# Three edits to a planned hybrid decoder kernel: at most four rows of x loaded ahead, a lead for the states' transposes, and head sums as two one-pass products

## The chip, the cores and the metric

The kernel runs on one core of a Trainium2 chip. A core has a matrix engine (TensorE, PE in the profile, with its weight loads as PEld), a vector engine (VectorE, DVE), an activation engine (ScalarE, ACT), a general engine (GpSimd, POOL), and a queue from which this kernel issues all its DMAs (SyncE, SP). The metric is the time of one execution in microseconds (us) on the device.

## What is computed

One layer of a hybrid decoder step, for a prompt of 1024 tokens and for 8 sample tokens with states of their own, with D = 1024:

```python
p = x @ w_in                                  # 1024 -> 3088 (GLA) + 4224 (RWKV) + 2048 (gates)
# GLA: 4 heads, keys of 128, values of 256: gated linear attention, norm, silu gate
S_t = diag(a_t) S_{t-1} + k_t^T v_t ; o_t = q_t S_t
# RWKV-7: 16 heads of 64, on p shifted by one token
kk = kb * k_k ; kk = kk / max(sqrt(sum(kk^2 over a head)), 1e-12)
S_t = S_{t-1} (diag(w_t) - kk_t^T (kk_t * a_t)) + v_t^T k_t ; y_t = S_t r_t
y = (y - mean(y)) * rsqrt(var(y) + eps) * lnx_w + lnx_b      # mean and variance over a head
bonus = sum(r * k * r_k over a head) * v
# merge
m = sigmoid(gate_a) * (o_gla @ w_up_gla) + sigmoid(gate_b) * (o_rwkv @ w_up_rwkv)
y_out = layernorm(alpha * x + m @ w_out)
```

Also returned are the states after the prompt, the samples' new states and the last projected rows. All tensors are float32.

## The kernel before, in words

The tokens are worked on in two passes of 520 (512 and the 8 samples, as two tiles of 260 columns) and 512 tokens. Activations lie feature by token: 128 features on the partitions, tokens along the columns. In each pass a plan of blocks runs through `w_in`, 128 output features a block: 8 slices of x by 3 products for each tile. Each float32 operand is split into a high part that TensorE takes in one pass (float32r) and the rest, and the products are high by high, high by low and low by high (`blocks`, L670 to L705). These are the products called `proj<-xh,whi`, `proj<-xl,whi` and `proj<-xh,wlo`, the input products of this text. Other products of full float32 operands go through TensorE in two passes, and the profile has two records for each.

After both passes come the products with `w_up_gla` and `w_up_rwkv` for each half, then `w_out` with the layer norm. At each of these changes of operand (a swap), the eight slices of x are replaced: `load_x` (L583) loads a slice into a buffer of the kind `row`, a cast on ScalarE makes the high part `xh` (`high`), a subtraction makes `xl` (`low`), and the row is freed. A slice can only be replaced after the last product that reads it, and the loads begin three blocks ahead (`AHEAD`). There are 26 `row` buffers of [128, 520] for everything: projected rows, GLA heads, RWKV pairs, samples, gates and x. A block that makes a projected row waits until a row is free beyond those that others wait for (`KEEP`, L57).

The RWKV heads are worked on in pairs, 8 a pass. A pair's `front` (L1027) makes decays, normalised keys, masked products (`big<-az,wide`) and the 32-step triangular solve on VectorE (`X`, `Xt`, over `LD` in DRAM); `back` and `turn` finish the inverse and transpose; `chain` (L1176) runs 8 dependent steps of small products (`pch<-wide,gg`, `pch<-rh,XT`, `pch<-wide`, and `pY`) with VectorE and ScalarE in between; `norm` (L1229) normalises. The sum over a head's 64 features is needed twice in `front` and twice in `norm`; `head_sums` (L461) is one float32 product with a block matrix of ones (`big<-row,cons`, 128 by 512). GLA heads (L752) do the same over 128 partitions with split operands already: `split` (L446) and `sums` (L453), the products `big<-part,onesr`. The samples' GLA states go through rows (`row<-state_gla`, `row<-vd`, stored as `gla_s`) and products `big<-row` of 8 columns (L886). The samples' RWKV step (L1249) begins with two transposes (`big<-cons,smp`); a pair's final state is transposed and stored by `state` (L1219, `big<-cons,Sp`).

The order is not written out by hand. Each piece of work is a stream, a generator of operations, and a planner (`run`, L357) picks operation after operation from all streams at build time: it prices each operation, keeps clocks for each engine and buffer, and takes the one with the lowest start time less a lead. The leads are the tables `PRIO` (engines other than TensorE) and `ON_PE` (L74 to L77). What comes out is one fixed order for each engine's queue; at run time each engine takes its queue strictly in order and waits on semaphores. So a late operand on one engine holds back all that stands behind it there.

Nearly all instructions go through one helper, so the profile gives them all the line L214; they are told apart by tile names.

Of the kernel before, what the change touches and what calls it, by code (L numbers as in the profile page):

```python
# [11 lines left out]
F32R = mybir.dt.float32r  # L12
# [8 lines left out]
P = 128  # L21
# [8 lines left out]
GH, GDK, GDV = 4, 128, 256  # L30
RH, RN = 16, 64
NPAIR = RH // 2
C = 64
# [22 lines left out]

KEEP = 1  # L57
AHEAD = 3
SPARE_ROWS = 8


# [12 lines left out]
PRIO = {"evacuate": 0.7, "pair": 0.4, "turn": 0.5, "chain": 0.5, "norm": 0.1, "x": 0.7, "lora": 0.2, "rank": -0.3,  # L74
        "head": 0.3, "gate": 0.05, "w": 0.3, "out": -0.1, "state": 0, "block": 0.0}
ON_PE = {"evacuate": 0.0, "pair": 0.15, "turn": 0.1, "chain": 0.15, "norm": 0.15, "x": 0.0, "lora": 0.15, "rank": 0.1,
         "head": 0.1, "gate": 0.06, "w": 0.0, "out": -0.03, "state": 0.0, "block": 0.0}  # L77

URGENT = 0.6
SIGMOID, EXP = "sigmoid_and_others", "natural_log_exp_and_others"  # L80
# [10 lines left out]

CST = {}
_o = 0
for _n, _w in [("ident", 128), ("gmask", 256), ("heads", 128)]:
    CST[_n] = (_o, _w)
    _o += _w
CST_W = _o
# [9 lines left out]
def constants():  # L107
    c = np.zeros((P, CST_W), np.float32)

    def put(name, v):  # L110
        o, w = CST[name]
        c[:, o:o + w] = v

    i = np.arange(P)
    put("ident", np.eye(P))
    put("heads", (i[:, None] // C) == (i[None] // C))
    s, t = i[:, None] % C, i[None, :] % C
    put("gmask", np.concatenate([s < t, s <= t], axis=1))
    lev = np.zeros((P, 64 * MASKED), np.float32)
    for n, m in enumerate(LEVELS[:MASKED]):  # L120
        ri = np.array([x for x in range(P) if (x // m) % 2 == 1])
        j = i[:, None]
        lev[:, 64 * n:64 * n + 64] = ((j // (2 * m)) == (ri[None, :] // (2 * m))) & ((j // m) % 2 == 0)
    return c, lev


class Op:
# [274 lines left out]
class Kern(Order):  # L402
# [57 lines left out]

    def head_sums(self, x):  # L461

        ps = yield from self.bank("big", [P, HT])
        yield self.P.matmul(ps, self.cst("heads"), x, start=True, stop=True)
        return ps

    def pvec(self, name, j):
# [4 lines left out]
    def setup(self):  # L472
        nc, a = self.nc, self.a
        E = mybir.EngineType
        self.es.enter_context(self.tc.manual_schedule(engines={E.PE, E.Activation, E.DVE, E.Pool, E.SP}))
        cp = self.pool("const")
        wp = self.pool("w", side="left")
        self.dr = self.pool("dr", space=DRAM)
        pp = self.pool("psum", space=PSUM)
        xp = self.pool("x", side="right")  # L480
        self.r1 = r1 = self.pool("work", side="left")
        for tag, bufs in BANKS.items():
            self.buffers(tag, bufs, lambda tag=tag, bufs=bufs: pp.tile([P, 512], F32, name=tag, bufs=bufs))
        for tag, (shape, bufs) in SBUF.items():
            dt = F32R if tag in PARTS else F32
            self.buffers(tag, bufs, lambda tag=tag, shape=shape, bufs=bufs, dt=dt:
                         r1.tile(shape, dt, name=tag, bufs=bufs))
        for tag, (shape, bufs) in WBUF.items():
            dt = F32 if tag == "wraw" else F32R
            self.buffers(tag, bufs, lambda tag=tag, shape=shape, bufs=bufs, dt=dt:  # L490
                         wp.tile(shape, dt, name=tag, bufs=bufs))
        for k in range(NK):
            for v in "hl":
                tag = f"x{v}{k}"
                self.buffers(tag, 1, lambda tag=tag: xp.tile([P, HALF], F32R, name=tag, bufs=1))
        nc.scalar.preload_act_table_set(EXP)
        self.cons = cp.tile([P, CST_W], F32, name="cons")
        self.pv = cp.tile([P, PV_W], F32, name="pv")
        self.ident = self.cst("ident")
        self.omu = cp.tile([P, NRC], F32, name="omu")  # L500
        self.oka = cp.tile([P, 8], F32, name="oka")
        self.nkk = cp.tile([P, 8], F32, name="nkk")
        self.bias = {}
        for n, v in [("glaeps", GLA_EPS), ("gneps", GN_EPS), ("lneps", LN_EPS), ("one", 1.0),
                     ("kkl", 0.5 * math.log(KK_SCALE))]:
            t = cp.tile([P, 1], F32, name="b_" + n)
            nc.vector.memset(t, v)
            self.bias[n] = t
        dbg = getattr(self, "dbg", {})
        self.o_gla = dbg.get("o_gla", None) or self.dr.tile([D, T], F32, name="o_gla")  # L510
        self.o_rwkv = dbg.get("o_rwkv", None) or self.dr.tile([D, T], F32, name="o_rwkv")
        self.sg = [[[self.dr.tile([P, PASS[i][1]], F32, name=f"sg{i}{n}{k}") for k in range(NK)] for n in range(2)]
                   for i in range(2)]
        self.mg = [[self.dr.tile([P, PASS[i][1]], F32, name=f"mg{i}{k}") for k in range(NK)] for i in range(2)]

        self.lev = cp.tile([P, 64 * MASKED], F32, name="lev")

        self.onesr = cp.tile([P, P], F32R, name="onesr")
        self.wa = cp.tile([P, NK * 16], F32, name="wa")
        self.alr = [cp.tile([96, HALF], F32R, name=f"alr{n}") for n in range(2)]  # L520
        self.gw2 = cp.tile([96, GH * GDK], F32R, name="gw2")
        self.GS = [cp.tile([P, GDV], F32, name=f"GS{h}") for h in range(GH)]

        self.smp = cp.tile([P, 4, NPAIR, NS], F32, name="smp")
        self.RS = self.dr.tile([4, NS, D], F32, name="RS")
        self.WA = self.dr.tile([2, NS, D], F32, name="WA")
        self.tail = cp.tile([P, NS + 1, NRC], F32, name="tail")
        self.carry = cp.tile([P, NRC], F32, name="carry")
        self.shT = cp.tile([P, NRC, NS], F32, name="shT")
        self.reset = cp.tile([P, HT], U8, name="reset")  # L530
        nc.vector.memset(self.reset, 1)
        nc.vector.memset(self.reset[:, ::C], 0)

        self.Sp = [cp.tile([P, C], F32, name=f"Sp{n}") for n in range(NPAIR)]
        for t in self.Sp:
            nc.gpsimd.memset(t, 0.0)

        for tag, n, bufs in (("az", 4 * HT, 2), ("XT", 2 * HT, 2), ("X1", HT, 1), ("As", 2 * HT, 1)):
            ts = [cp.tile([P, n], F32, name=f"{tag}{i}") for i in range(bufs)]
            for t in ts:  # L540
                nc.gpsimd.memset(t, 0.0)
            self.fixed(tag, ts)
# [9 lines left out]
    def load_constants(self):  # L552
        a, V, E = self.a, self.V, self.E
        yield from self.load("wa", self.S.dma_start(self.wa, a["wa"]))
        self.has.add("wa")
        row = yield from self.row()
        yield V.memset(row, 1.0)
        yield V.tensor_copy(self.onesr, row[:, :P])
        yield V.memset(row, 0.0)
        for t in self.alr:  # L560
            yield V.tensor_copy(t, row[0:96])
        self.has.add("alr")
        yield from self.load("pv", self.S.dma_start(self.pv, a["pv"]))
        yield from self.load("shift", self.S.dma_start(self.shT, a["shiftT"]))
        o = PV["mu"][0]
        yield V.tensor_scalar(self.omu, self.pv[:, o:o + NRC], -1.0, 1.0, ALU.mult, ALU.add)
        o = PV["ka"][0]
        yield V.tensor_scalar(self.oka, self.pv[:, o:o + 8], -1.0, 1.0, ALU.mult, ALU.add)
        o = PV["kk"][0]
        yield V.tensor_scalar(self.nkk, self.pv[:, o:o + 8], -1.0, None, ALU.mult)  # L570
        self.has.add("pv")
        yield from self.load("cst", self.S.dma_start(self.cons, a["cst"]))
        raw = row[0:96, :GH * GDK]
        for n in range(3):
            yield self.S.dma_start(raw[32 * n:32 * n + 16], a["gla_alpha_w2"])
        yield self.S.dma_start(self.lev, a["lev"])
        yield V.tensor_copy(self.gw2, raw)
        yield V.tensor_sub(self.gw2[64:96], raw[64:96], self.gw2[64:96].bitcast(F32))
        self.free(row)
        self.has.add("cst")  # L580


    def load_x(self, src, i, wait=None, low_rank=False):  # L583
# [25 lines left out]
        self.spawn(high(), "x")  # L609
        self.spawn(low(), "x")  # L610
        for k in range(NK):
            raw = yield from self.row(n)
            rows = slice(k * P, (k + 1) * P)
            yield from self.load(f"x{k}", self.S.dma_start(
                raw, src[k] if isinstance(src, list) else src[rows, base:base + n]))
            raws.append(raw)
# [996 lines left out]

def layout(i):
    f = np.ascontiguousarray
    cst, lev = constants()
    ch = lambda v: v.reshape(-1, P).T
    pv = np.concatenate([ch(i["rwkv_mu"][0]), ch(i["rwkv_w0"][0]), ch(i["rwkv_a0"][0]), ch(i["rwkv_k_k"][0]),
                         ch(i["rwkv_k_a"][0]), ch(i["rwkv_r_k"][0].reshape(-1)), ch(i["rwkv_lnx_w"][0]),
# [2 lines left out]
    x = np.concatenate([xp, xs], axis=0)  # L1622
    xT = f(np.concatenate([xp[:HT], xs, xp[HT:]], axis=0).T)
    return {
        "cst": cst, "lev": lev, "pv": f(pv), "xT": xT, "x": f(x), "w_in": f(i["w_in"][0]),
        "wa": f(i["w_in"][0][:, OFF_A:OFF_R].reshape(NK, P, 16).transpose(1, 0, 2).reshape(P, NK * 16)),
        "gla_alpha_w2": f(i["gla_alpha_w2"][0]), "state_gla": f(i["state_gla"]), "state_rwkv": f(i["state_rwkv"]),
        "shiftT": f(i["state_rwkv_shift"][0].reshape(NS, NRC, P).transpose(2, 1, 0)),
# [25 lines left out]
```

## Time and profile before

| what | us |
| --- | --- |
| median of 3 runs | 1686.61 |
| lowest and highest | 1685.98, 1691.09 |
| the profiled execution | 1687.94 |
| span of its instructions | 1686.2 |
| TensorE busy | 1628.7 |
| VectorE busy | 1184.6 |
| ScalarE busy | 830.7 |
| mean granted clock of TensorE | 0.986 |

In rows of groups of instructions stand the line, the engine, the operation, out<-in by the program's names, the tile's shape, the count, then the busy time in us, the mean ns of one, the idle time before them in us and what ended it. In rows of the timeline stand the start in us, the duration in us, the engine, the instruction, and in brackets the idle time of the engine before it and what ended that. A product's duration covers its whole way through the array, so neighbours overlap; what a product costs in a stream is the distance from its start to the next one's. `f32` stands in the rows for both kinds of float32. The granted clock is a share of full speed.

### The profile page before, as it was taken

The numbers are of one execution on the slowest core, as the hardware profiler recorded it, in microseconds if no ns is written. First come the engines' busy times: TensorE is split into PE (matmuls) and PEld (weight loads), VectorE is DVE, ScalarE is ACT, GpSimd is POOL, SyncE is SP. The second block draws the span as 40 slices with busy tenths as digits, with TensorE's granted clock in tenths as the row PEclk, the third lists the DMA queues.
The fourth block names the chain that finished last, engine by engine and source line by source line (L and its number), as shares of the span: only waits on it lengthen the run. The fifth ranks groups of instructions, "written<-read, shape, count | busy, mean of one in ns | idle before, by whom it ended". The sixth has DMA issues, their size and how long they took to land.

```text
span 1686.2 us, 29927 instructions
## 1 busy us (share of the span) xinstructions
PE 1628.7 (97%) x10322; PEld 1430.9 (85%) x10322; DVE 1184.6 (70%) x3114; ACT 830.7 (49%) x1974; POOL 86.0 (5%) x183
## 2 busy tenths in 40 slices
PE   8999999999999998999999999999989999999998
PEld 7899999999999996888878778778867889988786
DVE  6777876887688766757656477898728876656565
ACT  5456755664657465443634254526243656644210
POOL 1100000100000000000000000200000000000000
PEclk9999999999999999899999999999988999999999
DMA  9777675777587657545364625454642487788522
GB/s 291 246 228 231 217 215 152 227 246 218 160 245 228 216 158 237 170 119 174 101 206 123 186 73 176 152 163 156 202 145 67 114 275 221 236 278 278 182 78 87
DMA packets 311778, 315.26 MB, mean 187 GB/s; under 512 B 75347, under 2 KB 197084, under 8 KB 311628
## 3 DMA queue, kind: packets, MB, share of 16 engines
q1 hardware_dynamic: 311628, 313.36, 59.9%
q8 instruction: 82, 1.34, 0.3%
q14 instruction: 68, 0.56, 0.1%
HBM read 195.45 MB, written 117.82 MB: 186 GB/s over the span
## 4 chain that ended last, share of the span: by engine, by line
PE 73%; DVE 12%; DMA 7%; ACT 3%; issue 2%; SPq 2%; POOL 0%; POOLq 0%; DVEq 0%; ACTq 0%
PE proj L214 41%; PE big L214 21%; PE pY L214 7%; DVE row L214 4%; PE pch L214 4%; DMA wide<-LD 2%; SPq L214 2%; DVE X L214 2%; DVE Xt L214 2%; ACT row L214 1%; DVE wide L214 1%; DMA row<-state_rwkv 1%; DVE wlo L214 1%; DVE az L214 1%; DMA wraw<-w_up_gla 1%
## 5 line engine op out<-in xcount | busy, mean ns | idle before, releaser
L214 PE MATMUL proj<-xl,whi 128*128 128x260 f32 (+1 forms) x1928 | 637.5, 331 | 0.0
L214 PE MATMUL proj<-xh,whi 128*128 128x260 f32 (+1 forms) x1928 | 635.9, 330 | 0.0
L214 PE MATMUL proj<-xh,wlo 128*128 128x260 f32 (+1 forms) x1928 | 635.0, 329 | 0.0
L214 PEld LDWEIGHTS proj<-xh,wlo 128*128 128x128 f32 x1928 | 364.9, 189 | 29.9 <-issue 6.6
L214 PEld LDWEIGHTS proj<-xh,whi 128*128 128x128 f32 x1928 | 365.2, 189 | 28.5 <-issue 5.4
L214 PEld LDWEIGHTS proj<-xl,whi 128*128 128x128 f32 x1928 | 364.9, 189 | 28.6 <-issue 6.5
L214 DVE TENSOR_TENSOR row<-row 128x256 f32<-128x256 f32 (+6 forms) x326 | 161.7, 503 | 23.8 <-ACT row L214 11.8
L214 ACT CAST whi<-wraw 128x512 fp32r<-128x512 f32 x210 | 129.9, 622 | 95.7 <-PE proj L214 51.7
L214 DVE TENSOR_TENSOR wlo<-wraw,whi 128x512 fp32r<-128x512 f32 x205 | 141.0, 691 | 40.5 <-ACT whi L214 37.3
L214 ACT ACTIVATE row<-row 128x512 f32<-128x512 f32 (+4 forms) x229 | 138.4, 611 | 44.6 <-DVE row L214 26.3
L214 DVE TENSOR_TENSOR Xt<-X,wide 128x60 f32<-128x60 f32 (+24 forms) x496 | 105.4, 212 | 43.8 <-DMA wide<-LD 31.2
L214 ACT ACTIVATE row<-proj,omu 128x260 f32<-128x260 f32 (+1 forms) x99 | 54.1, 547 | 150.2 <-PE proj L214 149.9
L214 PE MATMUL big<-row 128*128 128x64 f32 (+4 forms) x712 | 115.6, 282 | 12.5 <-DVE row L214 11.5
L214 PEld LDWEIGHTS big<-row 128*128 128x128 f32 (+1 forms) x712 | 96.9, 193 | 23.3 <-DVE row L214 13.5
L214 ACT ACTIVATE s0p<-wide,pc 64x64 f32<-64x64 f32 x256 | 88.1, 344 | 52.7 <-DVE wide L214 48.5
L214 DVE TENSOR_TENSOR X<-X,Xt 128x60 f32<-128x60 f32 (+24 forms) x496 | 104.8, 211 | 11.9
L214 ACT COPY wide<-pch 64x64 f32<-64x64 f32 x221 | 45.5, 206 | 114.3 <-PE pch L214 110.4
L214 DVE SCALAR_TENSOR_TENSOR row<-proj,pv,row 128x259 f32<-128x259 f32 (+1 forms) x99 | 56.3, 569 | 49.7 <-ACT tail L214 33.7
L214 DVE SCALAR_TENSOR_TENSOR wide<-pch,pc,s0p 64x64 f32<-64x64 f32 x224 | 63.1, 282 | 38.3 <-PE pch L214 33.7
L214 POOL TENSOR_TENSOR row<-row 128x512 f32<-128x512 f32 (+7 forms) x43 | 45.5, 1059 | 794.4 <-ACT row L214 211.7
L214 ACT COPY row<-big 128x128 f32<-128x128 f32 (+7 forms) x165 | 46.7, 307 | 66.8 <-PE big L214 63.5
L381 ACT ACT_TABLE_LOAD x56 | 71.8, 1283 | 1.0
(254 smaller groups left out, 2560.6 us busy)
## 6 DMA issues: line engine op xcount, KB each, us to landing
wraw<-w_in SPq DMA_DIRECT2D x146, 256.0 KB
wh<-whi SPq DMA_DIRECT2D x146, 256.0 KB
wl<-wlo SPq DMA_DIRECT2D x146, 256.0 KB
whi<-wh SPq DMA_DIRECT2D x146, 256.0 KB
wlo<-wl SPq DMA_DIRECT2D x146, 256.0 KB
wide<-LD SPq DMA_DIRECT2D x64, 128.0 KB
wraw<-w_up_gla SPq DMA_DIRECT2D x32, 256.0 KB
wraw<-w_up_rwkv SPq DMA_DIRECT2D x32, 256.0 KB
```

What stands on the lines that cost most here:

```text
L214: ways.append((eng, lambda call=call: call(out, *args, **kw), price(eng, name, out, args, ins)))
L381: self.nc.scalar.preload_act_table_set(self.table)
```

## The change

Three edits.

First, `load_x` loads a row of x only while fewer than `RAWS` = 4 rows are loaded and not yet cast; the first load of all, at the start of pass 0, is exempt. Second, `ON_PE["state"]` goes from 0.0 to 0.1, which gives the streams `state`, `rwkv_sample` and `tails` a lead of 0.1 us on TensorE. Third, `head_sums` splits its operand into the two `part` buffers and forms the sum as two one-pass products with a block matrix of ones in float32r, `headsr`, which comes by a load of its own at the start.

```diff
+RAWS = 4
...
-         "head": 0.1, "gate": 0.06, "w": 0.0, "out": -0.03, "state": 0.0, "block": 0.0}
+         "head": 0.1, "gate": 0.06, "w": 0.0, "out": -0.03, "state": 0.1, "block": 0.0}
...
-for _n, _w in [("ident", 128), ("gmask", 256), ("heads", 128)]:
+for _n, _w in [("ident", 128), ("gmask", 256)]:
...
     def head_sums(self, x):
 
+        hi, lo = yield from self.split(x)
         ps = yield from self.bank("big", [P, HT])
-        yield self.P.matmul(ps, self.cst("heads"), x, start=True, stop=True)
+        yield from self.sums(ps, self.headsr, hi, lo)
+        self.free(hi, lo)
         return ps
...
-        raw = row[0:96, :GH * GDK]
+        raw, heads = row[0:96, :GH * GDK], (yield from self.row(P))
+        yield self.S.dma_start(heads, a["heads"])
...
-        self.free(row)
+        yield V.tensor_copy(self.headsr, heads)
+        self.free(row, heads)
...
         for k in range(NK):
+            yield lambda: k - len(his) < RAWS or low_rank and not i
             raw = yield from self.row(n)
```

Since the planner weighs all streams at every step, the order of all engines shifts from the first head sum on. Three places follow.

On TensorE in pass 1, before: a run of products without an input product, with the second transpose of the samples at its head, chain steps (`pch`, `pY`), one head sum (`big<-row,cons`) and the masked products of the next pair (`big<-az,wide`).

```order
L214 MATMUL proj<-xh_9626,wlo 128x512
L214 MATMUL big<-cons,smp 128x128
L214 MATMUL pY<-gg,wide 128x128
L214 MATMUL pch<-wide,gg 128x128
L214 MATMUL pY<-az_175,wide 128x128
L214 MATMUL pch<-rh,XT_179 128x128
L214 MATMUL pch<-wide 128x128
L214 MATMUL big<-row,cons 128x512
L214 MATMUL pY<-gg,wide 128x128
L214 MATMUL pch<-wide,gg 128x128
L214 MATMUL big<-az_176,wide 128x256
```

Now, on TensorE at the place where the samples' transposes stand: the two products of a head sum (`big<-part,headsr`) with input products between them, masked products between the chain steps, and the second transpose among input products.

```order
L215 MATMUL big<-part,headsr 128x512
L215 MATMUL proj<-xh_9650,wlo 128x512
L215 MATMUL proj<-xh_9659,whi 128x512
L215 MATMUL big<-part,headsr 128x512
L215 MATMUL proj<-xl_9668,whi 128x512
L215 MATMUL big<-az_177,wide 128x256
L215 MATMUL pY<-gg,wide 128x128
L215 MATMUL big<-az_177,wide 128x256
L215 MATMUL pch<-wide,gg 128x128
```

The sum became two rows with two input products between; the samples' transposes moved some 400 input products towards the front.

On TensorE near the end of pass 0, before: the last products of the GLA samples (`big<-row`, 8 columns).

```order
L214 MATMUL proj<-xl_292,whi 128x260
L214 MATMUL proj<-xh_280,wlo 128x260
L214 MATMUL proj<-xh_285,whi 128x260
L214 MATMUL proj<-xl_313,whi 128x260
L214 MATMUL proj<-xh_285,wlo 128x260
L214 MATMUL big<-row 128x8 x8
L214 MATMUL proj<-xh_198,whi 128x260
```

Now, one of the same kind on TensorE:

```order
L215 MATMUL proj<-xl_254,whi 128x260
L215 MATMUL big<-row 128x8 x2
L215 MATMUL proj<-xh_235,wlo 128x260
L215 MATMUL proj<-xh_241,whi 128x260
L215 MATMUL proj<-xl_256,whi 128x260
L215 MATMUL proj<-xh_241,wlo 128x260
L215 MATMUL proj<-xh_248,whi 128x260
L215 MATMUL proj<-xl_289,whi 128x260
L215 MATMUL proj<-xh_248,wlo 128x260
```

Eight sample products in one row became pairs with input products between them.

On SP at the swap to the first half of `o_gla`, before: the loads of x (`row<-o_gla`) stand far ahead of the store of the gate row `sg_122`, which is the next row after these.

```order
L214 DMA row<-o_gla 128x520 x8
L214 DMA LD_15816<-gg 32x8x32 x3
L214 DMA whi<-wh_1_9190 128x512
L214 DMA wlo<-wl_1_9223 128x512
L214 DMA whi<-wh_0_9345 128x512
L214 DMA wlo<-wl_0_9347 128x512
L214 DMA whi<-wh_1_9367 128x512
L214 DMA wlo<-wl_1_9369 128x512
L214 DMA wraw<-w_up_gla 128x4x128 x3
L214 DMA wide<-LD_15816 32x1024 x4
L214 DMA o_gla<-row 128x512 x2
L214 DMA row<-sg_92 128x520
```

Now, on SP at the same swap, the second four of them:

```order
L215 DMA LD_16310<-gg 32x8x32 x4
L215 DMA wraw<-w_up_gla 128x4x128
L215 DMA shift_p<-sto 33x128
L215 DMA row<-sg_93 128x520
L215 DMA wide<-LD_16310 32x1024
L215 DMA sg_122<-row 128x512
L215 DMA wide<-LD_16310 32x1024
L215 DMA row<-o_gla 128x520 x3
L215 DMA wide<-LD_16310 32x1024 x2
L215 DMA wraw<-w_up_gla 128x4x128
L215 DMA row<-o_gla 128x520
```

The last four rows of x moved behind the gate row's store and two of the loads of LD.

More of the change, by code (lines that the diff above doesn't have):

```diff
@@ L115, in constants @@
     put("ident", np.eye(P))
-    put("heads", (i[:, None] // C) == (i[None] // C))
     s, t = i[:, None] % C, i[None, :] % C
@@ L123, in constants @@
         lev[:, 64 * n:64 * n + 64] = ((j // (2 * m)) == (ri[None, :] // (2 * m))) & ((j // m) % 2 == 0)
-    return c, lev
+    return c, lev, ((i[:, None] // C) == (i[None] // C)).astype(np.float32)
 class Op:
@@ L518, in setup @@
         self.onesr = cp.tile([P, P], F32R, name="onesr")
+        self.headsr = cp.tile([P, P], F32R, name="headsr")
         self.wa = cp.tile([P, NK * 16], F32, name="wa")
@@ L1615, in layout @@
     f = np.ascontiguousarray
-    cst, lev = constants()
+    cst, lev, heads = constants()
     ch = lambda v: v.reshape(-1, P).T
@@ L1624, in layout @@
     return {
-        "cst": cst, "lev": lev, "pv": f(pv), "xT": xT, "x": f(x), "w_in": f(i["w_in"][0]),
+        "cst": cst, "lev": lev, "heads": heads, "pv": f(pv), "xT": xT, "x": f(x), "w_in": f(i["w_in"][0]),
         "wa": f(i["w_in"][0][:, OFF_A:OFF_R].reshape(NK, P, 16).transpose(1, 0, 2).reshape(P, NK * 16)),
```

## The prediction

> **What bounds the kernel now.** I read the page first: its engine row, then the slices.
>
> ```profile
> span 1686.2 us, 29927 instructions
> PE 1628.7 (97%) x10322; PEld 1430.9 (85%) x10322; DVE 1184.6 (70%) x3114; ACT 830.7 (49%) x1974; POOL 86.0 (5%) x183
> PE   8999999999999998999999999999989999999998
> PEclk9999999999999999899999999999988999999999
> DMA  9777675777587657545364625454642487788522
> ```
>
> TensorE (PE) is busy 97% of the span, nothing else more than 85%, and PE's nines run from start to end, so the time is PE's work plus the few places where PE waits or runs slowly. Busy shares of PE hide the second part, because its products overlap, so I looked for places where the granted clock falls (it does so only after waits) and asked for the busy times there, first of everything, then of products into `proj` alone. Columns: stretch, its length, busy us of PE, PEld, DVE, ACT, POOL with counts, granted clock, DMA share, GB/s.
>
> ```profile
> 670.40:686.40 16.00, 9.12 (x42) 8.62 (x41) 13.73 (x57) 6.10 (x14) 0.00 (x0) 0.57 0.38 129
> 962.30:978.60 16.30, 13.54 (x73) 10.84 (x71) 5.66 (x10) 8.57 (x17) 0.00 (x0) 0.79 0.15 41
> 985.10:998.40 13.30, 10.85 (x55) 8.91 (x54) 12.54 (x25) 5.45 (x14) 3.21 (x7) 0.87 0.34 96
> 1238.00:1254.10 16.10, 13.01 (x56) 9.64 (x55) 3.18 (x6) 6.57 (x13) 0.00 (x0) 0.68 0.19 58
> 1260.70:1277.40 16.70, 11.68 (x43) 8.64 (x43) 14.44 (x28) 7.33 (x19) 0.07 (x1) 0.69 0.14 47
> ```
>
> ```profile
> 962.30:978.60 16.30, 0.23 (x2) 0.08 (x1) 0.00 (x0) 0.60 (x1) 0.79 0.15 41
> 1260.70:1277.40 16.70, 0.33 (x2) 0.23 (x2) 0.00 (x0) 0.59 (x1) 0.69 0.14 47
> ```
>
> These five stretches are 78.4 us long and PE is idle for 78.4 - 58.2 = 20.2 us of it. The lost clock, length times (1 - clock), is 6.9 + 3.4 + 1.7 + 5.2 + 5.2 = 22.4 us more. Not all of that counts, since the clock is also low while PE is idle: the stretches cost between 20 and 42 us. The second answer says why four of them exist: PE has no products of the input with the weights to put between the dependent steps (2 in 16 us each), and steps on the serial chain stand bare:
>
> ```profile
> 1262.52 0.49 PE L214 MATMUL pch<-rh,XT 128*128 128x128 f32 x2 [0.62 <-DVE rh L214]
> 1264.14 0.49 PE L214 MATMUL pch<-wide 128*128 128x128 f32 x2 [1.14 <-ACT wide L214]
> ...
> 1265.73 0.46 PE L214 MATMUL pch<-wide,gg 128*128 128x128 f32 x2 [0.88 <-DVE wide L214]
> ```
>
> The first stretch is another thing. PE's fixed order holds eight products of the GLA samples in a row, and the samples' states had been issued only just before:
>
> ```profile
> 671.00 0.48 SPq L214 DMA_DIRECT2D row<-vd  x1
> 674.76 0.91 ACT L214 ACTIVATE row<-row 128x256 f32<-128x256 f32 x2 [2.09 <-DMA row<-vd]
> 676.22 1.02 PE L214 MATMUL big<-row 128*128 128x8 f32 x4 [5.49 <-DVE row L214]
> ```
>
> **The change, part by part.** The sum is made against the profiled execution's own time, 1687.94 us, which is 1.33 us above the median of the runs (1686.61).
>
> *The sums over a head.* There are 64 of them (4 for each of 8 pairs in 2 passes), one f32 product each, which the profile records as two passes:
>
> ```profile
> L214 PE MATMUL big<-row,cons 128*128 128x512 f32 x128 | 69.7, 629 | 2.4 <-ACT row L214 1.1 <-DVE row L214 1.1
> ```
>
> The 629 ns overlap with their neighbours, so the price is read from starts:
>
> ```profile
> 933.36 0.40 PE L214 MATMUL proj<-xh,wlo 128*128 128x512 f32 x1
> 933.59 0.39 PE L214 MATMUL proj<-xh,whi 128*128 128x512 f32 x1
> 933.83 0.39 PE L214 MATMUL proj<-xl,whi 128*128 128x512 f32 x1
> 934.05 1.02 PE L214 MATMUL big<-row,cons 128*128 128x512 f32 x2
> 934.51 0.80 PE L214 MATMUL proj<-xh,wlo 128*128 128x512 f32 x1
> 935.14 0.39 PE L214 MATMUL proj<-xh,whi 128*128 128x512 f32 x1
> ```
>
> A one-pass product of 512 columns takes 0.23 us from start to start (933.36, 933.59, 933.83). From 934.05 to 935.14 lie one sum and one such product, so the sum takes 1.09 - 0.23 = 0.86 us. Its replacement has the form of the GLA heads' sums, for which a start-to-start step is on record as well:
>
> ```profile
> 814.35 0.40 PE L214 MATMUL big<-part,onesr 128*128 128x512 f32 x1
> 814.59 0.38 PE L214 MATMUL pch<-rh,XT 128*128 128x128 f32 x2
> ```
>
> That is 0.24 us; two are 0.47. Each sum frees 0.39 us of PE, 64 of them 25 us. PE is full nearly everywhere, so I book all of it: **-25**.
>
> *The splits that feed them.* Each sum now needs a cast and a subtraction first:
>
> ```profile
> L214 ACT CAST part<-row x5: 615/628/642, 172.9 to 1561.3; 128x520 fp32r<-128x520 f32 x3, 128x512 fp32r<-128x512 f32 x2
> L214 DVE CAST part<-row x5: 420/426/429, 683.9 to 1319.0; 128x512 fp32r<-128x512 f32 x4, 128x520 fp32r<-128x520 f32 x1
> L214 DVE TENSOR_TENSOR part<-row,part x8: 684/690/694, 174.4 to 1319.7; 128x520 fp32r<-128x520 f32 x4, 128x512 fp32r<-128x512 f32 x4
> ```
>
> The cast goes about half to ScalarE (0.63 us) and half to VectorE (0.43), the subtraction (0.69) almost always to VectorE. That is at most 64 x 0.69 + 32 x 0.43 = 58 us on VectorE and 32 x 0.63 = 20 us on ScalarE. VectorE goes from 70% to about 76%, ScalarE from 49% to about 52%; neither becomes the bound, and PE's products are the cover. What is exposed is the wait of PE, whose order is fixed, for the second part: between nothing and, with no product in between, 64 x 0.69 = 44 us. The nearest row is the one above: 128 passes that wait for a row in just the same way lost 2.4 us. The changed order puts about two products of the input (0.47 us) between the two halves of a sum. I take **+3**, at most +10. By an estimate from these rows (cast, subtraction, two products and handing over) a sum holds the two `part` buffers for some 3 us, 64 times in 1640 us, so they are mostly free. One more load and one copy at the start go beside the first loads of weights, and the constant block is smaller by as much: nothing.
>
> *Few rows of x wait; the states' transposes.* Before, eight rows of 26 were filled well ahead of each swap of x; now four are, and the rows so spared are free for the streams that feed PE. And the two transposes of the RWKV samples, which before were put off until PE had run dry, now stand some 400 input products earlier in PE's order:
>
> ```profile
> 985.10 0.27 PE L214 MATMUL big<-cons,smp 128*128 128x128 f32 x1
> ```
>
> In that order the five stretches are gone. The eight sample products in a row became pairs with input products between; the longest runs without an input product in pass 1 are down from 45, 38 and 27 products to 18, and chain steps in them are covered by products of `az` or stand alone at most twice. Bounds: 0 (new places of the same kind) to -42. A run of mostly independent products stands in the old order too, and PE waited for nothing in it:
>
> ```profile
> 655.50 1.03 PE L214 MATMUL big<-row,wa 128*16 128x512 f32 x2
> 656.47 1.13 PE L214 MATMUL big<-az,wide 128*128 128x256 f32 x4
> 657.43 0.38 PE L214 MATMUL pch<-wide 128*128 128x128 f32 x2
> ```
>
> I take **-30**: most of the 42, with 12 kept for new bare places, which an order planned from estimates will have somewhere.
>
> Here the trace and a page part. In the stretch at 985 us the longest single wait of PE is short, yet its clock is 0.87:
>
> ```profile
> 989.47 1.55 PE L214 MATMUL big<-row,cons 128*128 128x512 f32 x2 [1.10 <-DVE row L214]
> ```
>
> So several waits of a microsecond are enough, and short bare runs of the new order could still cost clock; that is a reason for the 12. The Trainium skill, "TensorE: Matmul & The Clock Gate", section "Part 1: The HAM clock gate", has the clock fall to half only after about 3.4 us of idling; by it the new order, with no such gap in sight, would keep none of the 12 and the sum would be 12 us lower. This row speaks against that.
>
> *What the spared rows cost.* The second four rows of x are now issued only when the first parts of x are being replaced, behind whatever stands ahead of them in SP's queue. At the swap to `o_gla` they stand behind the store of a gate row and two loads of LD:
>
> ```profile
> 1367.31 0.32 SPq L214 DMA_DIRECT2D sg<-row  x1
> 1369.25 0.37 PE L214 MATMUL big<-xh,whi 128*128 128x260 f32 x1
> ```
>
> That store was issued 1.9 us before PE took up the new x. A load of such a size needs 3.8 us (671.00 to 674.76 above), then 0.6 and 0.7 us of splitting: row 4 is ready about 3.2 us after the swap. It is needed after 12 products of 260 columns, 0.12 us each:
>
> ```profile
> 668.67 0.28 PE L214 MATMUL proj<-xh,whi 128*128 128x260 f32 x1
> 668.79 0.28 PE L214 MATMUL proj<-xl,whi 128*128 128x260 f32 x1
> ```
>
> so at 1.4 us: some 2 us of wait, 3 with the later rows. The swap between the two upward products of the first half, from 260 columns to 260, has 24 x 0.12 = 2.9 us of warning against the 5.1 us of load and split: 1.5 us. At the swap to pass 1 the second rows stand behind the last stores of sample states and four reloads of weights: 1.5 us too, by estimate. The other swaps run into 512 columns or out of them, where 12 products give 2.8 us and 24 give 5.6: nothing. **+6**, from 0 to +9.
>
> The sum: -25 + 3 - 30 + 6 = **-46**; 1687.94 - 46 = 1641.9, or 1640.6 against the median. I say **1641**.
>
> **The rivals.** *New bare stretches of the same size.* The order is planned with fixed prices, and the old one had five places where reality differed; the new one may have its own. Then the -30 falls away: -25 + 3 + 6 = -16, 1672. For it: such places lie in every pass. Against: the shorter runs in the order. Chance 0.14.
>
> *Weight loads set the pace.* Each sum has two loads before and after, at this price:
>
> ```profile
> L214 PEld LDWEIGHTS proj<-xh,wlo 128*128 128x128 f32 x1928 | 364.9, 189 | 29.9 <-issue 6.6
> ```
>
> If they did, the sums would free nothing: 3 - 30 + 6 = -21, 1667. This is how the Trainium skill, "Perfetto Trace Analysis", section "Identifying the Most-Contended Engine", would have TensorE judged: by the loads' busy share, matmul busy time being no good measure. Against it: 0.86 us for a sum with two loads of 0.19. Chance 0.05.
>
> *Slower: PE waits at every sum.* PE takes its order strictly. If the planned cover is spent by the time a sum comes, each sum costs a bare cast and subtraction, 0.63 + 0.69 = 1.32 us, 84 us in all: -25 - 30 + 6 + 84 = +35, 1723. It decides from (25 + 30 - 6) / 64 = 0.77 us of wait for a sum. For it: the splits queue on VectorE among 0.2 us steps of the triangular solves. Against: 2.4 us of wait in 128 passes now. Chance 0.05.
>
> That the change does not act can be left out: the order shows all three parts.
>
> **How the numbers follow.** Forecast 0.76, at 1641. The best end takes all 42 and no cost: 1688 - 67 = 1621. The other end keeps a third of the stretches' gain and has the higher costs: -25 - 14 + 9 + 7 = -23, 1665. So 1622 to 1665, which leaves out the slower rival and most of the other two, about 2 in 10. Faster by over 0.3% (5 us, about what a measurement of this kernel can tell) 0.93; within it 0.03, from the first two rivals with further losses; slower 0.04.
>
> **What would show it.** Right: `big<-part,headsr` 128 times at about 390 ns with steps of 0.23; PE waiting less than 10 us for `part`; no stretch of more than 10 us without `proj`, and a granted clock near 1.00 between 600 and 1300 us; waits of 1 to 3 us on `xl` at three swaps. Wrong: PE idle by 0.7 us before the sums; a clock as low as 0.9 in any 100 us of pass 1; a span that fell by 25 us alone.

## The result and the profile after

The changed kernel takes 1649.79 us (median of 4 runs, 1647.24 to 1653.32), against 1687.66 for the kernel before in the same call. The ratio is 0.9775, with a 95% interval of 0.9750 to 0.9799: 38 us faster (34 to 42). The prediction said 1641 and 1622 to 1665. The profiled execution took 1649.76 us, 38.2 less than the one of before.

The head of the page of the changed kernel, to be set beside the one in the prediction:

```profile
span 1647.8 us, 30094 instructions
PE 1604.5 (97%) x10322; PEld 1422.9 (86%) x10322; DVE 1234.7 (75%) x3187; ACT 844.6 (51%) x2015; POOL 103.3 (6%) x192
PE   8999999999999999999999999999999999999998
PEclk9999999999999999999999999999999999999999
```

The eights in the granted clock are gone, and PE's share of the span is the same 97%. VectorE has 50 us more to do, in a span that is 38 us shorter.

Two stretches show where most of the gain came from: 665 to 695 us holds the first of the five bare stretches, 900 to 1300 us the other four. Busy times of before first (columns as in the prediction), then of after:

```profile
665.00:695.00 30.00, 23.12 (x146) 21.33 (x145) 21.69 (x80) 16.40 (x34) 0.00 (x0) 0.77 0.50 148
900.00:1300.00 400.00, 381.57 (x1957) 314.26 (x1955) 281.39 (x782) 166.74 (x413) 29.50 (x49) 0.96 0.48 146
```

```profile
665.00:695.00 30.00, 29.29 (x168) 21.80 (x167) 24.07 (x80) 15.58 (x35) 1.28 (x1) 1.00 0.69 215
900.00:1300.00 400.00, 391.65 (x2133) 328.02 (x2133) 307.72 (x860) 195.58 (x473) 32.59 (x50) 1.00 0.49 151
```

In the first, PE's idle time fell from 6.9 to 0.7 us and the lost clock, length times (1 - clock), from 6.9 us to none. In the second, idle time fell from 18.4 to 8.4 us and lost clock from 16 to under 2. In the two passes no stretch without an input product is longer than 6.3 us any more (it lies at 617 us, and PE is busy all through it); the five bare ones of before were 10.8 to 16.4 us long.

The head sums, by tile, in the changed kernel:

```profile
L215 PE MATMUL big<-part,headsr x128: 387/400/579, 49.9 to 1428.6; 128*128 128x512 f32 x128
L215 DVE TENSOR_TENSOR part<-row,part x63: 680/692/1014, 48.6 to 1427.9; 128x512 fp32r<-128x512 f32 x59, 128x520 fp32r<-128x520 f32 x4
L215 POOL TENSOR_TENSOR part<-row,part x9: 1269/1286/2260, 196.8 to 1161.4; 128x512 fp32r<-128x512 f32 x9
```

And one pair of them in the timeline:

```profile
49.86 0.63 PE L215 MATMUL big<-part,headsr 128*128 128x512 f32 x2
50.33 0.28 PE L215 MATMUL proj<-xh,wlo 128*128 128x260 f32 x1
```

The two take 0.47 us to the next start (49.86 to 50.33), as the prediction priced them. What PE waits for at the parts hardly shows in PE's own waits (1.3 us in all). It shows in those of the weight loads: a load for a head sum reads `headsr` alone, yet the profile has it wait for the part that the product behind it reads. From the waits of the changed kernel by what was waited for, with total, times and longest:

```profile
PEld pch L215 <- DVE rh L215: 13.1, 27, 1.1
PEld big L215 <- DVE row L215: 11.9, 18, 1.9
...
PEld big L215 <- DVE part L215: 3.8, 15, 0.7
...
PEld big L215 <- ACT row L215: 1.9, 4, 0.7
...
PEld big L215 <- ACT part L215: 1.5, 4, 0.4
...
PEld big L215 <- POOL part L215: 1.1, 2, 1.0
```

That is 6.4 us for the parts, in 21 waits.

### The profile page after: what moved, and what is told of

It reads as the page before. It is cut to its first block, busy times and chain, and to the rows that moved or that the text cites. A ratio compares the mean times of both kernels' runs of the same rounds, so it can differ in the third digit from the quotient of the medians.

```text
span 1647.8 us, 30094 instructions
## 1 busy us (share of the span) xinstructions
PE 1604.5 (97%) x10322; PEld 1422.9 (86%) x10322; DVE 1234.7 (75%) x3187; ACT 844.6 (51%) x2015; POOL 103.3 (6%) x192
## 4 chain that ended last, share of the span: by engine, by line
PE 71%; DVE 13%; DMA 7%; ACT 3%; SPq 3%; issue 2%; POOL 0%; POOLq 0%; DVEq 0%; ACTq 0%
PE proj L215 39%; PE big L215 22%; PE pY L215 7%; PE pch L215 4%; DVE row L215 4%; SPq L215 3%; DVE X L215 2%; DVE Xt L215 2%; DMA wide<-LD 2%; ACT row L215 1%; DVE wide L215 1%; DVE wlo L215 1%; DVE pair L215 1%; DMA whi<-wh 1%; DMA l2s<-lora 1%
## 5 line engine op out<-in xcount | busy, mean ns | idle before, releaser
L215 PE MATMUL proj<-xh,whi 128*128 128x260 f32 (+1 forms) x1872 | 618.2, 330 | 0.1
L215 PE MATMUL proj<-xh,wlo 128*128 128x260 f32 (+1 forms) x1872 | 615.8, 329 | 0.5 <-POOL wlo L215 0.5
L215 PE MATMUL proj<-xl,whi 128*128 128x260 f32 (+1 forms) x1872 | 612.9, 327 | 0.8 <-DVE xl L215 0.7
L215 PEld LDWEIGHTS proj<-xh,wlo 128*128 128x128 f32 x1872 | 354.0, 189 | 28.0 <-issue 5.6
L215 PEld LDWEIGHTS proj<-xh,whi 128*128 128x128 f32 x1872 | 354.7, 189 | 24.7 <-issue 2.3
L215 PEld LDWEIGHTS proj<-xl,whi 128*128 128x128 f32 x1872 | 354.4, 189 | 24.8 <-issue 1.7
L215 DVE TENSOR_TENSOR row<-row 128x512 f32<-128x512 f32 (+10 forms) x329 | 164.6, 505 | 11.5 <-PE big L215 4.5
L215 ACT ACTIVATE row<-row 128x512 f32<-128x512 f32 (+5 forms) x229 | 138.5, 610 | 33.2 <-DVE row L215 21.1
L215 POOL TENSOR_TENSOR row<-row 128x512 f32<-128x512 f32 (+5 forms) x40 | 47.9, 1198 | 715.2 <-ACT row L215 210.8
L215 PE MATMUL big<-az,wide 128*128 128x256 f32 x256 | 66.7, 383 | 0.3 <-DVE gg L215 0.2
```

What stands on the lines that cost most here:

```text
L215: ways.append((eng, lambda call=call: call(out, *args, **kw), price(eng, name, out, args, ins)))
```

## Theories

*Blocked banks* (formed after the result, from the orders; theory A in the expectations). The streams `state` and `rwkv_sample` take one of the three `big` banks first and then wait for their transpose on PE. With a lead of 0.0 that transpose loses against any input product that is ready. For a final transpose the planner's code says why: it uses a smaller tile of the array, for which the planner adds 0.09 us (`SWITCH`), so a lead of 0.1 is just enough to win (`SWITCH` itself was not varied). A stream can thus sit on a bank for tens of microseconds. When three do so, no stream that needs a `big` bank can go on; the planner places input products until rows run out, and then PE has only the dependent steps (that the rows run out is read from the planner's code, and no trace shows it). By this the lead of 0.1, not the limit on rows of x, removed the four stretches of pass 1. The trace of before fits it. Products into `big` alone, in the 50 us ahead of the stretch at 1238, of before and then of after:

```profile
1188.00:1237.90 49.90, 0.00 (x0) 0.11 (x1) 0.69 (x1) 0.00 (x0) 1.00 0.73 226
```

```profile
1188.00:1237.90 49.90, 12.56 (x69) 9.76 (x69) 4.14 (x6) 6.05 (x13) 1.00 0.50 148
```

And what stands at the head of the stretch at 962 us and at the end of these 50 us, in before:

```profile
962.32 0.27 PE L214 MATMUL big<-cons,smp 128*128 128x128 f32 x1
962.42 0.38 PE L214 MATMUL big<-cons,Sp 128*64 128x128 f32 x2
...
1237.73 0.39 PE L214 MATMUL proj<-xh,wlo 128*128 128x512 f32 x1
1237.96 0.49 PE L214 MATMUL big<-cons,Sp 128*64 128x128 f32 x3
```

Not one product wrote a `big` bank for 49.9 us; then three final transposes came together, and with them the banks were free. At 962 us it was one transpose of the samples and two final ones, after 27 us. The gap alone is not the sign: the faster kernels have gaps of 20 to 34 us too (s_only one of 33.5 us ahead of 1212 us), with no bare stretch behind. The three transposes that end it are the sign.

*Spared rows* (the prediction's; theory B): the limit on raw rows of x leaves rows to the streams that feed PE, and the samples' transposes come earlier.

## The experiments

All ratios are to the kernel before, run in the same call; 0.01 is 17 us.

| kernel | head sums | limit | lead | median us | ratio (95%) |
| --- | --- | --- | --- | --- | --- |
| s_only | | | yes | 1668.91 | 0.9897 (0.9861 to 0.9933) |
| r_only | | yes | | 1679.82 | 0.9962 (0.9946 to 0.9979) |
| h_only | yes | | | 1703.72 | 1.0118 (1.0077 to 1.0158) |
| hs | yes | | yes | 1660.03 | 0.9848 (0.9832 to 0.9865) |
| rs | | yes | yes | 1661.24 | 0.9855 (0.9834 to 0.9875) |
| changed | yes | yes | yes | 1649.79 | 0.9775 (0.9750 to 0.9799) |
| smp_lead | | | samples and tails | 1703.94 | 1.0112 (1.0095 to 1.0128) |
| smp_lead_bank | | | the same, bank rule | 1660.77 | 0.9857 (0.9842 to 0.9872) |
| lead_free | | yes | the same, bank rule | 1652.71 | 0.9795 (0.9778 to 0.9811) |
| all_bank | yes | yes | the same, bank rule | 1649.38 | 0.9777 (0.9763 to 0.9792) |
| r_pass1 | yes | at pass 1 | yes | 1651.74 | 0.9804 (0.9781 to 0.9827) |
| twice | yes, one product more | yes | yes | 1654.36 | 0.9808 (0.9781 to 0.9835) |
| short_sub | yes, cut | yes | yes | 1642.34 | 0.9737 (0.9720 to 0.9754) |

### One edit alone

s_only, the lead alone:

```diff
-         "head": 0.1, "gate": 0.06, "w": 0.0, "out": -0.03, "state": 0.0, "block": 0.0}
+         "head": 0.1, "gate": 0.06, "w": 0.0, "out": -0.03, "state": 0.1, "block": 0.0}
```

> The kernel before with the lead of the state streams alone (0.0 to 0.1). Theory A (three state or sample streams that have taken all three big banks and whose transposes are put off block every other stream, rows run out, and PE stands bare): the four bare stretches of pass 1 (962, 985, 1238, 1260 us in the kernel before) go, about 25 us: 1655 to 1665. Theory B (the prediction's: the rows spared by the limit on raw rows of x feed PE): this edit alone leaves most of the stretches: 1680 to 1690.

r_only, the limit alone:

```diff
+RAWS = 4
...
         for k in range(NK):
+            yield lambda: k - len(his) < RAWS or low_rank and not i
```

> The kernel before with the limit of four raw rows of x alone. Theory A (blocked big banks): the four stretches of pass 1 stay, the one at 670 us may shrink, the swaps of x gain waits of 1 to 3 us: 1680 to 1692. Theory B (spared rows feed PE): the stretches shrink by some 30 us: 1655 to 1665.

h_only, the head sums alone:

```diff
+        hi, lo = yield from self.split(x)
         ps = yield from self.bank("big", [P, HT])
-        yield self.P.matmul(ps, self.cst("heads"), x, start=True, stop=True)
+        yield from self.sums(ps, self.headsr, hi, lo)
+        self.free(hi, lo)
...
```

> The kernel before with the two one-pass products for each head sum alone. By PE's work alone: 64 x 0.39 = 25 us less, 1660 to 1665. Theory A: the banks are still blocked, and the longest runs without an input product in this order are 50, 37, 42 and 69 products in place of 45, 27, 38 and 21, so 5 to 20 us of the 25 are lost again: 1667 to 1685. If weight loads set PE's pace: 1685 to 1690.

The lead alone gave 17 us (11 to 23), the limit alone 6 (4 to 9), and the head sums alone cost 20 (13 to 27). The same two stretches tell which edit does what. First s_only, then r_only:

```profile
665.00:695.00 30.00, 23.11 (x143) 20.30 (x143) 20.52 (x77) 15.13 (x30) 0.00 (x0) 0.83 0.47 143
900.00:1300.00 400.00, 391.54 (x2092) 324.37 (x2091) 297.01 (x833) 180.72 (x447) 30.60 (x49) 0.99 0.50 151
```

```profile
665.00:695.00 30.00, 29.64 (x177) 22.15 (x176) 22.06 (x74) 16.78 (x35) 1.42 (x2) 1.00 0.76 246
900.00:1300.00 400.00, 383.55 (x1962) 314.96 (x1960) 290.78 (x806) 166.54 (x410) 29.23 (x49) 0.96 0.48 147
```

The lead cures pass 1 (clock 0.96 to 0.99, idle 18.4 to 8.5 us) and leaves 665 to 695 much as it was (idle 6.9 us in both); the limit cures 665 to 695 (idle 6.9 to 0.4 us, clock 0.77 to 1.00) and leaves pass 1 much as it was (idle 16.5 us, clock 0.96). These two edits have stretches of their own, and the prediction booked all five in one sum. s_only's 1668.9 us lies 4 us above the range for blocked banks and 11 below the one for spared rows. r_only and h_only fell outside what blocked banks said too: r_only by a hair on the good side, h_only by 19 us on the bad one, where I had 1667 to 1685. In h_only longer bare stretches cost more than the sums saved: by the starts in its trace PE has no input product for 16.8, 19.2, 18.3, 13.5 and 38.9 us (at 665, 957, 989, 1160 and 1328 us). Ahead of the last no product wrote a `big` bank for 23.4 us, and then the samples' last transpose and two final ones came together:

```profile
1304.00:1327.40 23.40, 0.00 (x0) 0.00 (x0) 0.59 (x1) 0.00 (x0) 1.00 0.66 211
```

```profile
1327.49 0.27 PE L215 MATMUL big<-cons,row 64*128 64x64 f32 x1
1327.70 0.41 PE L215 MATMUL big<-cons,Sp 128*64 128x128 f32 x2
```

How the limit removes the stretch at 670 us, r_only shows in part. The last states of the samples are loaded no earlier there (at 672.09 us, against 671.00 before), but input products now fill the time until they are ready, where before PE stood idle for 5.49 us:

```profile
677.46 0.61 PE L216 MATMUL big<-row 128*128 128x8 f32 x4 [0.36 <-DVE row L216]
```

That fits rows left free for the blocks. That it is the rows, and not another shift of the order, was not tried by itself.

### Two edits at a time

hs, the changed kernel without the limit:

```diff
         for k in range(NK):
-            yield lambda: k - len(his) < RAWS or low_rank and not i
```

> The changed kernel without the limit on raw rows of x (head sums and lead of the states kept). Theory A (blocked big banks): no bare stretch comes back in pass 1; at the swaps of x the 6 us of waits go, the eight sample products in a row near 670 us may come back (10 us): 1640 to 1660. Theory B (spared rows): the stretches come back, 1670 to 1682.

rs, the changed kernel with the old head sums:

```diff
-        hi, lo = yield from self.split(x)
         ps = yield from self.bank("big", [P, HT])
-        yield from self.sums(ps, self.headsr, hi, lo)
-        self.free(hi, lo)
+        yield self.P.matmul(ps, self.cst("heads"), x, start=True, stop=True)
...
```

> The changed kernel without the new head sums (limit on raw rows and lead of the states kept). If the sums are worth all of their 64 x 0.39 = 25 us of PE's work: 1672 to 1677. If about two thirds of that come back as small waits, as the kernel with the doubled product and the pair with and without sums say (5 of 15 us, 8 of 25 us): 1655 to 1661.

hs is 26 us faster than before, rs 24 us. Without the limit the stretch at 665 to 695 is back and pass 1 stays whole, the other way round from what spared rows would do. From hs:

```profile
665.00:695.00 30.00, 21.50 (x134) 19.14 (x133) 23.16 (x88) 11.95 (x32) 0.00 (x0) 0.77 0.35 110
900.00:1300.00 400.00, 392.67 (x2145) 329.47 (x2144) 316.63 (x874) 191.23 (x467) 35.10 (x57) 1.00 0.49 152
```

### Banks or lead

smp_lead gives the lead to the samples and tails alone; the final transposes become a kind `final` with 0.0:

```diff
...
-         "head": 0.1, "gate": 0.06, "w": 0.0, "out": -0.03, "state": 0.0, "block": 0.0}
+         "head": 0.1, "gate": 0.06, "w": 0.0, "out": -0.03, "state": 0.1, "final": 0.0, "block": 0.0}
...
-            self.spawn(self.state(p, S), "state")
+            self.spawn(self.state(p, S), "final")
```

> The kernel before, with the lead of 0.1 for the samples' transposes and the tails alone; the final transposes of the states keep 0.0. In this order three of them still stand together in pass 1, twice, behind runs of 63 products without an input product. Theory A (blocked big banks): two long bare stretches in pass 1, no gain or a loss: 1680 to 1705. If what counts is that the samples' transposes come early (the prediction's second reason): 1655 to 1668.

smp_lead_bank adds one rule, that such a transpose takes its bank only when all three are free:

```diff
-    def bank(self, tag, shape):
...
-        x = yield from self.get(tag)
+    def bank(self, tag, shape, keep=0):
...
+        x = yield from self.get(tag, 1, keep)
...
     def state(self, p, S):
-        pt = yield from self.bank("big", [C, P])
+        pt = yield from self.bank("big", [C, P], 2)
```

> As smp_lead, but a state's final transpose takes its big bank only when all three are free, so that never three wait holding them. Its lead stays 0.0. Theory A (blocked big banks): the stretches of pass 1 go as with the lead: 1652 to 1668. If the lead itself is what counts: as smp_lead, 1680 to 1705.

This pair is the sharpest. smp_lead is 19 us slower than before (16 to 22), smp_lead_bank 24 us faster (22 to 27), and the one edit between them is when a bank is taken. Products into `big` in the 40 us ahead of 1059.6 us, in smp_lead and then in smp_lead_bank:

```profile
1020.00:1059.60 39.60, 0.00 (x0) 0.11 (x1) 0.69 (x1) 0.00 (x0) 1.00 0.74 225
```

```profile
1020.00:1059.60 39.60, 9.38 (x53) 7.31 (x54) 2.35 (x4) 3.16 (x7) 1.00 0.63 202
```

And all work just after, again smp_lead first:

```profile
1060.00:1095.00 35.00, 25.23 (x96) 18.29 (x95) 22.94 (x45) 18.40 (x43) 3.07 (x3) 0.67 0.12 36
```

```profile
1060.00:1095.00 35.00, 33.93 (x181) 27.92 (x180) 28.64 (x93) 15.66 (x44) 5.96 (x10) 1.00 0.53 169
```

The final transposes of smp_lead_bank come as late as the planner likes (the first at 1343 us, 284 us after smp_lead's), with no bare stretch in pass 1; the one at 670 us stays, as the limit is not there. So early final transposes are not what counts, and early samples' transposes are not enough; the banks decide. Two more kernels use the same rule and leads: lead_free is the same with the limit (old head sums); all_bank is the changed kernel with this rule, and lead 0.0 for `final`.

```diff
+RAWS = 4
...
+            yield lambda: k - len(his) < RAWS or low_rank and not i
...
+        pt = yield from self.bank("big", [C, P], 2)
```

> The kernel before with the limit on raw rows, and the rule that a state's final transpose takes its big bank only when all three are free; those transposes keep the lead 0.0, the samples' have 0.1; old head sums. Theory A (blocked big banks in pass 1, the lump of eight sample products at 670 us removed by the limit): 1687 - 24 - 12 = 1651, 1646 to 1658. If the limit and the banks work on the same stretches: 1660 or more.

> The changed kernel with the same rule on the big banks in place of the lead for the final transposes (head sums and limit kept). Theory A: the lead does nothing else than to keep the banks from being blocked, so the time is that of the changed kernel, 1644 to 1654. If the early transposes themselves are worth something: 1655 to 1665.

Both came out as blocked banks said: 35 us faster than before (32 to 37), and 38 (35 to 40), the time of the changed kernel. So with the bank rule the final transposes need no lead.

### What the head sums are worth

twice issues the first product of each head sum two times, the second overwriting the first:

```diff
-        yield from self.sums(ps, self.headsr, hi, lo)
+        op = self.P.matmul(ps, self.headsr, hi, start=True, stop=False)
+        extra, once = self.P.matmul(ps, self.headsr, hi, start=True, stop=True).fn, op.fn
+        op.fn = lambda: (extra(), once())
...
+        yield self.P.matmul(ps, self.headsr, lo, start=False, stop=True)
```

> The changed kernel with the first of the two products of each head sum issued twice (the second overwrites the first), 64 one-pass products more, in the same order otherwise. If PE's products set the time one for one, 64 x 0.23 = 15 us more than the changed kernel: 1662 to 1667. If the freed time of PE is mostly given back in waits: 0 to 5 us more, 1650 to 1655.

The 15 us of added work cost 5 us (4.6 by the medians, 5.4 by the spans). The intervals of the two ratios overlap: by them the cost is 6 us give or take 6. So 15 us is out, and some two thirds went into time in which PE would have waited, a share that may be as small as a fifth or as large as all.

short_sub keeps the order, leaves the second part out of the sums and cuts the subtraction to 64 of 512 columns:

```diff
-        hi, lo = yield from self.split(x)
...
+        part = eng.tensor_sub(lo[:, :64], x[:, :64], hi[:, :64].bitcast(F32))
...
-        yield from self.sums(ps, self.headsr, hi, lo)
+        yield self.P.matmul(ps, self.headsr, hi, start=True, stop=False)
...
+        op.fn = self.P.matmul(ps, self.headsr, hi, start=False, stop=True).fn
...
```

> The changed kernel in the same order, with the subtraction of each head sum's split cut to 64 of its 512 columns, and the second product reading the first part again (the second part is left out of the sum). VectorE has some 64 x 0.6 = 38 us less to do, PE the same. If the splits' time on VectorE is why most of the 25 us came back as waits: 1630 to 1642. If the waits are for steps of the serial chain that the splits do not hold up: 1646 to 1652.

It is 7 us faster than the changed kernel (7.4 by the medians, 6.4 give or take 5 by the ratios), between the two expectations. The weight loads' waits for the parts, in short_sub and then in twice:

```profile
PEld big L215 <- ACT part L215: 0.7, 2, 0.4
...
PEld big L215 <- DVE part L215: 0.6, 3, 0.2
```

```profile
PEld big L215 <- DVE part L215: 0.9, 3, 0.5
...
PEld big L215 <- ACT part L215: 0.8, 3, 0.3
```

The 6.4 us fell to 1.3 and 1.7 us. If these waits reached PE in full, they are 5.1 of the 7 us that short_sub gained, and 4.7 us of what hid the added product in twice; no run shows what share of them reached PE. VectorE itself had 30 us less to do in short_sub (1234.7 to 1204.8) and GpSimd 9, not the 38 expected of VectorE, and the time fell by 7: the splits' work is mostly beside PE's.

The three pairs with and without the new head sums, each at the same lead and limit, differ by 8 us (s_only to hs), 13 (rs to changed) and 3 (lead_free to all_bank), each give or take 4 to 7, never by 25. In rs, the weight loads waited less for `rh` of the chain and for rows written by VectorE, and more for rows written by ScalarE:

```profile
PEld big L216 <- DVE row L216: 8.5, 16, 1.3
PEld pch L216 <- DVE rh L216: 7.6, 23, 1.0
PEld big L216 <- ACT row L216: 5.3, 13, 0.6
```

From rs to changed, that is +3.4 and +5.5 and -3.4 us, and +6.4 for the parts. But these rows are a choice out of some thirty. All waits of the weight loads that are put down to an engine or a DMA grew by 4 us only (56.8 to 60.9), those put down to "issue" fell by 24 (47.7 to 23.6), and PE's own grew by 4 (30.8 to 34.5). So the balance does not close, and it stays open where the other 12 of the 25 us went. A part of it can be read from the starts in the trace of the changed kernel: from the start of each of the 128 products to the start of what follows it on PE, they take 37.5 us, 0.29 us each, where steps of 0.235 us would take 30.

### The late rows of x

r_pass1 keeps the limit only for the load for pass 1:

```diff
-            yield lambda: k - len(his) < RAWS or low_rank and not i
+            yield lambda: k - len(his) < RAWS or not (low_rank and i)
```

> The changed kernel with the limit on raw rows kept only at the swap to pass 1. If the waits at the swaps to o_gla (1330 us) and o_rwkv (1390 us) come from the late second four rows, some 6 us go: 1641 to 1647. If they are what any swap costs: 1648 to 1653.

1651.74 us against 1649.79: no gain. PE's waits for `xh` and `xl` were 4.1 us in the changed kernel (the weight loads' 8.4):

```profile
PE pY L215 <- ACT xh L215: 1.8, 2, 1.2
PE pY L215 <- DVE xl L215: 1.6, 4, 0.6
...
PE proj L215 <- DVE xl L215: 0.7, 2, 0.3
```

In r_pass1 they are 1.0 us (the weight loads' 3.0), but a wait of 2.9 us for a weight stands there instead:

```profile
PE pY L215 <- ACT whi L215: 2.9, 1, 2.9
PE big L215 <- DVE xl L215: 0.6, 1, 0.6
...
PE pY L215 <- DVE xl L215: 0.4, 1, 0.4
```

Whether that wait follows from the earlier loads of x was not tried.

## Why the prediction was right, and where its steps were not

*The sign and the bound* were right: time lay in PE's work and in a few bare stretches, and both fell. The signs that it named came: `big<-part,headsr` 128 times at 400 ns, a granted clock of 1.00 between 600 and 1300 us, no stretch of over 10 us without input products in the passes. Waits for `xh` and `xl` came, none longer than 1.2 us at PE, against the 1 to 3 us at three swaps that it named.

*The stretches and the late rows*, -30 + 6 = -24 in the prediction, measured 24 us (21 to 28) in rs: the size was right. That needed no right reason, since the -30 was read from the length and clock of the stretches themselves, whatever made them. The reason was half wrong. "The rows so spared are free for the streams that feed PE" can hold for the stretch at 670 us alone, which goes with the limit and comes back without it. The four stretches of pass 1 do not care for the limit; they go with the lead or with the rule on banks. The prediction saw that the samples' transposes moved, and took it for a second reason beside the rows; it did not ask what those streams hold while they are put off. Why each pair of stretches has a second one, 15 to 20 us after the first (985 and 1260 us), was not tried by itself; both parts of a pair came and went together.

*The head sums* were mis-sized. "PE is full nearly everywhere, so I book all of it" is the step that failed: the forecast had -25 and +3 for the splits, 22 us together, and 3 to 13 arrived, depending on what else was in the kernel; alone they made it 20 us slower, with longer bare stretches in the replanned order. With the 13 us of the full change, this is the 9 us between the 1641 of the forecast and the 1650 measured. PE's 97% counts products that overlap: one of 0.40 us whose successor can start after 0.23 us hides up to 0.17 us of wait. That the rest of the saving went into such hidden waits fits twice, but is not shown.

*The splits' waits*, +3 and at most +10: 6.4 us by the weight loads, about 6 to 7 us by short_sub. The prediction's nearest row, 2.4 us in 128 passes, counted PE's waits alone and left out those of the loads (PEld).

*The late x*, +6: 4.1 us of waits at PE, of which removing most gave nothing. One of its terms was also added up wrong: 5.1 us of load and split against 2.9 us of warning leave 2.2 us, not 1.5.

*The rivals.* New bare stretches of the old size did not come. (Four of the old five were in the planned order itself, which has no input product there; they were not places where the chip differed from the plan.) PE does not wait at every sum: 6.4 us over 64 sums is 0.1 us each, far from 0.77. Weight loads do not set the pace by themselves: their number is the same in rs and in the changed kernel, so by that rival the sums would free nothing, and they freed 13 us (8 to 19). The rule of the Trainium skill, "TensorE: Matmul & The Clock Gate", section "Part 1: The HAM clock gate", that the clock falls after about 3.4 us of idling, does not fit what is measured here. PE's longest wait for another engine in 1238 to 1254 us of before is 0.8 us, at a granted clock of 0.68:

```profile
PE big L214 <- ACT As L214: 0.8, 1, 0.8
PE big L214 <- ACT XT L214: 0.8, 1, 0.8
PE big L214 <- DVE wide L214: 0.8, 1, 0.8
```

## What to carry to other kernels

Before crediting a new order to the buffers that an edit frees, list what each stream holds while its next operation is put off: a stream of low precedence that has taken a shared bank blocks streams of high precedence, and the sign in a trace is a long time without any product into that bank, ended by several of the low ones together. Undo each part alone before naming causes: here two edits owned different stretches, and the third was a loss by itself. And price saved work on an engine that is 97% busy by an experiment that adds a little of it back or takes the edit out; here a microsecond of added products cost about a third of a microsecond, and a saved one was worth about half, both with wide intervals.

## What was not expected of the hardware

The clock falls in stretches in which PE is busy for most of the time: in smp_lead it is 0.67 over 35 us in which PE was busy for 25.2. In that kernel the two such stretches alone account for 35 x 0.33 + 35 x 0.29 = 22 us of lost clock, by length times (1 - clock), beside 21 us of idle time (busy time grows as the clock falls, so the two are not apart):

```profile
1330.00:1365.00 35.00, 23.79 (x99) 17.06 (x97) 21.83 (x37) 17.39 (x39) 3.69 (x7) 0.71 0.28 85
```

One short wait seems to be enough. In the changed kernel PE waits 1.48 us at 923.6 us; by the clock's records it then has half the clock from 927.0 us on for 3.4 us, and a product takes 0.63 in place of 0.40 us:

```profile
925.08 1.11 PE L215 MATMUL big<-row 128*128 128x64 f32 x8 [1.48 <-DVE row L215]
...
926.55 0.40 PE L215 MATMUL proj<-xh,whi 128*128 128x512 f32 x1
...
927.02 0.63 PE L215 MATMUL proj<-xh,wlo 128*128 128x512 f32 x1
```

In the records of these traces the clock is either full or one half, and a low spell lasts 3.4 us or a multiple of it (but for the last of each, which the end cuts off): in before, 13.7, 6.8, 3.4, 10.2 and 10.2 us in the five stretches. So the 0.57 to 0.87 read there are mixtures of the two.

A full float32 product of 128 by 512 has two records in the profile, but it holds PE for 0.86 us, nearly four times the 0.23 us of a one-pass product.

A subtraction for a split that goes to GpSimd takes 1286 ns, against 692 on VectorE; nine went there, and the longest took 2260 ns (spans on GpSimd are rough in this profile).
